# A recurrent layer whose heads run as two chains of 64x64 products, with the modulation beside them

## The chip, the cores and the metric

The kernel runs on one core of one Trainium2 chip. The metric is the device time of one execution in microseconds (us). A core has TensorE (PE in the profile, its weight loads PEld), VectorE (DVE), ScalarE (ACT), GpSimd (POOL) and SyncE (SP), which here issues the transfers (DMA).

## The reference

`reference(...)` runs two blocks one behind the other on 256 tokens of width 1024, in fp32. The first has four layers, each a mixer followed by a gated projection of a side input `p[i]` and a layer norm; the mixers are a short convolution, a state-space layer (S5), the recurrent layer (RWKV-7) and a convolution again. The recurrent layer, with 16 heads of 64, is the one that changes:

```
def _rwkv_step(state, inp):
    r_t, w_t, k_t, v_t, kk_t, a_t = inp
    sa = jnp.einsum("bhvk,bhk->bhv", state, -kk_t)
    state = (state * w_t[:, :, None, :] + sa[..., None] * (kk_t * a_t)[:, :, None, :]
             + v_t[..., None] * k_t[:, :, None, :])
    out = jnp.einsum("bhvk,bhk->bhv", state, r_t)
    return state, out
```

Before it come the projections r, k, v and the low-rank paths for decay and `a`; behind it a norm per head, a bonus term, a gate `silu(z)` and the output product.

The second block has two layers over two streams, the tokens (the first block's output) and a context of 256 rows, which has a feed-forward network (FFN), mixers with attention, and an FFN again. Shifts, scales and gates of both streams come from the **modulation**:

```
        mod_x = jnp.split(jax.nn.silu(c) @ ada_w[l] + ada_b[l], N_MOD, axis=-1)
        mod_c = jnp.split(jax.nn.silu(c_ctx)[None, :] @ ada_w[l] + ada_b[l], N_MOD, axis=-1)
```

## The kernel before, in words

Activations lie transposed in SBUF, 128 channels on the partitions and 256 tokens along the row, in eight such pieces. A linear layer takes its weights in tiles of 128x1024 fp32, 512 KB each, in `get` (L600): SyncE fetches the tile, ScalarE rounds it (`whi`, L601) and VectorE takes the rest (`wlo`, L602); TensorE then runs three products for each 128x128 block, hi by hi, hi by lo, lo by hi, 24 matmuls of 256 columns for a tile. All TensorE products go through `matmul` (L433) or `transpose` (L437), all operations of VectorE and ScalarE but the splits through one helper (L403).

The order on every engine is fixed when the program is written out. Each stream is a Python generator that asks for a weight tile or says how long it would wait; `weave` holds two of them, X (the first block, then the tokens) and C (the context), keeps a model of the engines' times, and lets the stream go on whose operands the model has ready. So C's matmuls fill X's waits. `par` does the same among generators inside a stream. Beside the streams runs `side`, work that is due by the clock of the model, the modulation `ada` above all: for each of 168 tiles of the modulation's weights one transfer of 512 KB (L1376) and one multiplication with a sum along the row for each stream that wants it (L1379, output `junk`, 288 sums). Its core and the condition under which `weave` steps it:

```
while self.side is not None and not self.hold and self.next <= self.now() and (self.V.t < self.now() + SLACK or self.next < self.now() - LATE):
```

`hold` is raised in `square` at the last chunk of a stream's FFN and in the first block's norm, and lowered again in the norm that follows; while it stands, no modulation is issued. `drain` empties the side work on the spot.

The recurrent layer (`rwkv`) works on pairs of heads, two heads on 128 partitions, eight pairs, each in four chunks of 64 tokens. `heads(f)` is the generator for pair f; three run at once, each with its own buffers and its own PSUM tag (`ca`, `cb`, `mm`). For a pair, in order:

- the rates, keys and queries, scaled by the running decay, on VectorE and ScalarE; the r and key rows of each head go into `arz`, zeroed beforehand, so that the other head's 64 rows are zero and products can use all 128 rows (two column halves of PSUM for the two heads);
- the strict lower triangle `lt`, and an inverse `xi` built by doubling in six levels: `lt` by `xi`, copied to `t1` (ScalarE), the transposed inverse `xt` by `t1`, written into `xi` under a mask (VectorE), then `xi` transposed anew by a product with the identity and copied (ScalarE);
- for each of four chunks in sequence: q, xi q, the state, the output, each a product and a copy;
- the norm per head (two sums across partitions as 128x256 products) and the output.

Before the first pair `rwkv` drains the side work; behind the last it drains again and starts the rest of the modulation with a new `ada`.

Of the kernel before, what the change touches and what calls it, by code (L numbers as in the profile page):

```python
# [9 lines left out]
F32 = mybir.dt.float32  # L10
# [3 lines left out]
AF = mybir.ActivationFunctionType  # L14
# [72 lines left out]
def constants():  # L87
# [13 lines left out]
    strict, incl = (s_ < t_) * 1.0, (s_ <= t_) * 1.0  # L101
    c.add("p1mask", np.block([[strict, incl], [strict, incl]]))
    two = lambda m: np.kron(np.eye(2), m)
    c.add("ltmask", two(strict.T))
    c.add("eye", np.tile(np.eye(64), (2, 1)))
    for lv in range(6):
        b = 1 << lv
        m = (s_ // (2 * b) == t_ // (2 * b)) & (s_ // b % 2 == 0) & (t_ // b % 2 == 1)
        c.add(f"lv{lv}", np.tile(m * 1.0, (2, 1)))
    c.add("lvT0", two(((s_ == t_ + 1) & (s_ % 2 == 1)) * 1.0))  # L110
# [329 lines left out]
class Net:  # L440
# [624 lines left out]
    def rwkv(self, X):  # L1065
# [84 lines left out]
        self.drain()  # L1150
        for q in range(3):
            a = self.slot(2 * q, [2048], f"rw_a{q}") if q < 2 else self.big("rw_a2")[:, :2048]
            b = self.slot((1, 3, 10)[q], [2048], f"rw_b{q}")
            s_ = dict(arz=a[:, :1024], bk=a[:, 1024:1792], rate=a[:, 1792:2048], tag=("ca", "cb", "mm")[q])
            s_.update({n: b[:, 512 * i:512 * i + 512] for i, n in enumerate(("lt", "xi", "xt", "t1"))})
            G.memset(s_["arz"], 0.0)
            sets.append(s_)
        free = list(range(3))
# [3 lines left out]
        spare = lambda f: (sets[f % 3]["xi"][:, S:], sets[f % 3]["rate"])  # L1162
# [13 lines left out]
        rates(range(3))  # L1176

        def heads(f):

# [5 lines left out]
            (lw, cw), (ei, _), (kk, sq), (rn, ew) = (two(d[n]) for n in ("lt", "xi", "xt", "t1"))  # L1185
            kv, bt, bv = sq, rn, r[:, f]

# [16 lines left out]

            arz = d["arz"].rearrange("p (c a e t) -> p c a e t", c=4, a=2, e=2)
# [4 lines left out]
            if f % 3 == 2:  # L1210
                rates(range(f + 1, min(f + 4, NCH)))
            V.scalar_tensor_tensor(out=bk[:, :, 0], in0=ch(bt), scalar=0.5, in1=ch(ei), op0=MUL, op1=MUL)
            A.activation(out=bk[:, :, 2], in_=bk[:, :, 0], func=AF.Copy)
            V.tensor_tensor(out=bk[:, :, 1], in0=ch(kv), in1=ch(ei), op=MUL)
            wl = self.few.tile([128, 4], F32, name="wl", bufs=2)
            V.tensor_copy(out=wl, in_=ch(ew)[:, :, 63])
            for e in range(2):
                h = hd[e]
                V.scalar_tensor_tensor(out=arz[h, :, 0, e], in0=ch(kk)[h], scalar=-1.0, in1=ch(lw)[h], op0=MUL, op1=MUL)
                V.tensor_tensor(out=arz[h, :, 1, e], in0=ch(r[:, f])[h], in1=ch(ew)[h], op=MUL)  # L1220
# [3 lines left out]
            for c in range(4):  # L1224
                for e in range(2):
                    T.matmul(vt[hd[e], c * 64:c * 64 + 64], lhsT=svc(c)[:, hv[e]], rhs=self.c("ident")[:, hd[e]], start=True, stop=True)
# [4 lines left out]

            ab2 = lambda t: t.rearrange("p a s -> p (a s)")
            bks = lambda e, c: ab2(bk[:, c, 1 - e:3 - e])
            c4 = lambda t: t.rearrange("p (c t) -> p c t", c=4)
            cm_ = lambda n, k=128: self.c(n, k).unsqueeze(1).to_broadcast([128, 4, k])
            p1 = [c4(d["lt"]), c4(d["t1"])]

            lt, xt, xi, t1 = c4(d["lt"]), c4(d["xt"]), c4(d["xi"][:, :S]), c4(d["t1"][:, :S])
            e4 = lambda t: t.rearrange("p c (e s) -> p c e s", e=2)

            def both(out, f, g):

                for c in range(4):
                    for e in range(2):
                        T.matmul(out[hd[e], c * 64:c * 64 + 64], lhsT=f(c, e), rhs=g(c, e), start=True, stop=True)

            ps = pst()
            pp, pl = two(ps)
            both(pp, lambda c, e: arz[:, c, 0, e], lambda c, e: bk[:, c, 0])
            both(pl, lambda c, e: bk[:, c, 0], lambda c, e: arz[:, c, 0, e])  # L1250
            twice = c4(pp).unsqueeze(2).to_broadcast([128, 4, 2, 64])
            V.tensor_tensor(out=e4(lt), in0=twice, in1=e4(cm_("ltmask")), op=MUL)
            A.activation(out=xi, in_=cm_("eye", 64), func=AF.Copy)
            V.copy_predicated(out=xi, mask=cm_("lv0", 64).bitcast(I32), data=c4(pl))
            A.activation(out=xt, in_=cm_("ident"), func=AF.Copy)
            V.copy_predicated(out=e4(xt), mask=e4(cm_("lvT0")).bitcast(I32), data=twice)
            yield 2.0

            for lv in range(1, 6):
# [3 lines left out]
                yield 0.7  # L1263
                ps = pst()
                both(ps, lambda c, e: xt[:, c, hd[e]], lambda c, e: t1[:, c])
                V.copy_predicated(out=xi, mask=cm_(f"lv{lv}", 64).bitcast(I32), data=c4(ps[:, :S]))
                if lv == 5:
                    break
                yield 0.8
                ps = pst()  # L1270
                for c in range(4):
                    for e in range(2):
# [4 lines left out]
            for e in range(2):  # L1277
                ps = pst()
                for c in range(4):
                    T.matmul(ps[:, c * 128:c * 128 + 128], lhsT=bks(e, c), rhs=arz[:, c, :, e], start=True, stop=True)  # L1280
                V.tensor_tensor(out=p1[e], in0=c4(ps), in1=cm_("p1mask"), op=MUL)

            bkt = d["xt"].rearrange("p (c e t) -> p c e t", c=4, e=2)
            for e in range(2):
                ps = pst()
                for c in range(4):
                    T.transpose(ps[:, c * 64:c * 64 + 64], bks(e, c)[hd[e]], self.c("ident")[hd[e], hd[e]])
                A.activation(out=bkt[:, :, e], in_=c4(ps[:, :S]), func=AF.Copy)
            yield 0.5

            o = d["bk"][:, :S]
            ba, states = d["bk"][:, 256:320], [d["bk"][:, 320 + 64 * i:384 + 64 * i] for i in range(2)]
            state = None
# [679 lines left out]
```

## Time and profile before

| | |
|---|---|
| Median of 3 runs | 2889.77 us (2887.61 to 2893.28) |
| Profiled execution, its own time | 2890.76 us |
| Its span in the trace | 2889.0 us |
| TensorE busy | 2749.4 us, 95% |
| VectorE busy | 2134.0 us, 74% |
| ScalarE busy | 1606.4 us, 56% |
| HBM over the span | 161 GB/s |

The span is the trace's own length, and the execution's time is 1.76 us more. A matmul's end is modelled, so that neighbours overlap; what matters is when the next one starts. A row of the timeline is: start, duration, engine, line, operation, output and inputs with the tile, the count of merged instructions, and in brackets how long the engine had been idle and who ended that. `64*128` before a shape is the rows by columns of the array that a product takes.

### The profile page before, as it was taken

Reading aid. Unit: us, or ns where it says so; the run is one execution under the profiler, and the core shown is the slowest. Engines: PE = TensorE matmul, PEld = TensorE weight load, DVE = VectorE, ACT = ScalarE, POOL = GpSimd, SP = SyncE. Lnnn points to the kernel's source line nnn. Section 1 sums busy time; section 2 is a strip of 40 time slices with the busy share of each in tenths; the row PEclk is TensorE's granted clock in tenths of the full one; section 3 lists DMA queues with packets and bytes.
Section 4 is the critical chain, followed back from the end, with each engine's and each line's share of the span. In section 5 each row is a group of like instructions: output and inputs, shape, how many; then the busy total and the mean of one; then the engine's idle time right before and its main releaser. Section 6 shows DMA issues by size and latency. Waiting matters only on the chain.

```text
span 2889.0 us, 58552 instructions
## 1 busy us (share of the span) xinstructions
PE 2749.4 (95%) x23798; PEld 2604.6 (90%) x23798; DVE 2134.0 (74%) x3953; ACT 1606.4 (56%) x2976; POOL 14.8 (1%) x41
## 2 busy tenths in 40 slices
PE   8978799899999998999999999999999999999999
PEld 8967799778998998998999978999999999996999
DVE  8877777666688788899789887777855556676655
ACT  5455555766555465877666766445422234466443
POOL 0000000000000000000000000000000000000000
PEclk9989799999999999999999999999999999999999
DMA  7743355201586665666576644666543433222554
GB/s 270 238 165 110 108 167 175 82 17 40 163 269 226 220 197 167 209 215 203 182 226 195 199 130 155 203 225 194 180 142 125 139 117 103 89 82 65 161 182 139
DMA packets 132751, 467.53 MB, mean 162 GB/s; under 512 B 14720, under 2 KB 19072, under 8 KB 131840
## 3 DMA queue, kind: packets, MB, share of 16 engines
q1 hardware_dynamic: 132480, 463.78, 50.0%
q8 instruction: 187, 3.06, 0.4%
q14 instruction: 84, 0.69, 0.1%
HBM read 462.67 MB, written 1.05 MB: 161 GB/s over the span
## 4 chain that ended last, share of the span: by engine, by line
PE 72%; DVE 12%; DMA 7%; ACT 6%; issue 3%; SPq 0%; ACTq 0%; DVEq 0%
PE ps_mm L433 62%; PE ps_ca L433 5%; DMA w<-in_ada_dram 5%; DVE wlo L602 3%; PE ps_cb L433 2%; DVE junk L1379 2%; PE ps_st L433 2%; DVE ssm_m L403 2%; ACT whi L601 2%; DVE tc L403 1%; PE ps_cb L437 1%; ACT rw_b L403 1%; ACT L403 1%; ACT tc L403 1%; DMA w<-in_ab_in_dram 1%
## 5 line engine op out<-in xcount | busy, mean ns | idle before, releaser
L601 ACT ACTIVATE whi<-w 128x1024 fp32r<-128x1024 f32 (+1 forms) x687 | 715.9, 1043 | 740.2 <-PE ps_mm L433 488.1
L602 DVE TENSOR_TENSOR wlo<-w,whi 128x1024 fp32r<-128x1024 f32 (+1 forms) x687 | 825.6, 1203 | 239.2 <-ACT whi L601 236.8
L433 PE MATMUL ps_mm<-h_hi,whi 128*128 128x256 f32 x3024 | 873.1, 290 | 17.1 <-ACT h_hi L403 12.4
L433 PE MATMUL ps_mm<-h_hi,wlo 128*128 128x256 f32 x3024 | 859.5, 285 | 9.5 <-DVE wlo L602 9.5
L433 PE MATMUL ps_mm<-h_lo,whi 128*128 128x256 f32 x3024 | 856.5, 284 | 0.6 <-DVE h_lo L403 0.5
L433 PEld LDWEIGHTS ps_mm<-h_hi,whi 128*128 128x128 f32 x3024 | 573.6, 190 | 25.8 <-ACT h_hi L403 15.1
L433 PEld LDWEIGHTS ps_mm<-h_hi,wlo 128*128 128x128 f32 x3024 | 573.3, 190 | 12.2 <-DVE wlo L602 11.5
L433 PEld LDWEIGHTS ps_mm<-h_lo,whi 128*128 128x128 f32 x3024 | 577.5, 191 | 5.2 <-DVE h_lo L403 1.9
L1379 DVE SCALAR_TENSOR_TENSOR junk<-w,cond 128x1024 bf16<-128x1024 f32 x288 | 351.7, 1221 | 145.0 <-DMA w<-in_ada_dram 144.1
L433 PE MATMUL ps_mm<-d_hi,whi 128*128 128x256 f32 x1232 | 355.7, 289 | 4.1 <-DVE ctx L403 3.0
L433 PE MATMUL ps_mm<-d_hi,wlo 128*128 128x256 f32 x1232 | 350.4, 285 | 1.5 <-DVE wlo L602 1.5
L433 PE MATMUL ps_mm<-d_lo,whi 128*128 128x256 f32 x1232 | 349.2, 283 | 0.4 <-DVE d_lo L403 0.4
L433 PEld LDWEIGHTS ps_mm<-d_hi,whi 128*128 128x128 f32 x1232 | 232.3, 189 | 8.7 <-issue 5.7
L433 PEld LDWEIGHTS ps_mm<-d_lo,whi 128*128 128x128 f32 x1232 | 234.0, 190 | 3.4 <-issue 1.2
L433 PEld LDWEIGHTS ps_mm<-d_hi,wlo 128*128 128x128 f32 x1232 | 232.1, 189 | 2.8 <-DVE wlo L602 2.0
L403 DVE TENSOR_TENSOR td<-td,ps_mm 128x256 f32<-128x256 f32 x154 | 64.4, 418 | 70.0 <-PE ps_mm L433 68.9
L403 ACT ACTIVATE d_hi<-td 128x256 fp32r<-128x256 f32 x154 | 63.0, 409 | 89.5 <-DVE td L403 88.7
L403 ACT ACT_TABLE_LOAD x78 | 100.1, 1283 | 2.1 <-PEq L1964 0.7
L433 PE MATMUL ps_mm<-x_hi,whi 128*128 128x256 f32 x256 | 73.5, 287 | 12.0 <-ACT whi L601 12.0
L403 ACT ACTIVATE tc<-tc 128x256 f32<-128x256 f32 x182 | 75.1, 413 | 5.6 <-DVE tc L403 2.6
L433 PE MATMUL ps_mm<-xs_hi,whi 128*128 128x256 f32 x256 | 73.4, 288 | 4.8 <-ACT xs_hi L403 4.4
L403 ACT ACTIVATE td<-ps_mm 128x256 f32<-128x256 f32 x154 | 57.4, 374 | 32.9 <-PE ps_mm L433 32.3
(467 smaller groups left out, 5270.5 us busy)
## 6 DMA issues: line engine op xcount, KB each, us to landing
w<-in_ffn_in_dram SPq DMA_DIRECT2D x268, 512.0 KB, 4.2
w<-in_ada_dram SPq DMA_DIRECT2D x168, 512.0 KB, 4.3
w<-in_ffn_out_dram SPq DMA_DIRECT2D x96, 512.0 KB, 4.1
w<-in_conv_in_dram SPq DMA_DIRECT2D x64, 512.0 KB, 4.7
w<-in_ffn_out_dram SPq DMA_DIRECT2D x48, 384.0 KB, 3.1
w<-in_ab_in_dram SPq DMA_DIRECT2D x34, 512.0 KB, 4.4
w<-in_ple_gate_dram SPq DMA_DIRECT2D x32, 512.0 KB, 4.5
w<-in_conv_out_dram SPq DMA_DIRECT2D x16, 512.0 KB, 5.2
```

Source lines behind the costliest of these rows:

```text
L403: return f(**kw)
L433: self.t.matmul(out, lhsT=lhsT, rhs=rhs, start=start, stop=stop)
L437: self.t.transpose(out, in_, ident)
L601: nc.scalar.activation(out=hi[:, :n], in_=w[:, :n], func=AF.Copy)
L602: nc.vector.tensor_tensor(out=lo[:, :n], in0=w[:, :n], in1=hi[:, :n].bitcast(F32), op=ALU.subtract)
L1379: nc.vector.scalar_tensor_tensor(out=self.junk, in0=w, scalar=1.0, in1=cb[:, s], op0=ALU.mult, op1=ALU.mult, accum_out=m[:, t, s:s + 1])
```

## The change

- There are two sets of buffers and two heads' pairs at a time instead of three. `arz` with its zeros becomes `ar`, and every product of a pair takes a 64x64 quadrant (or 64x128) of the array, the head's own rows.
- The inverse is kept with its transpose: `x` is updated at each level by a second set of products, under masks `lvT0` to `lvT4`, and no product with the identity stands between levels.
- The four chunks' sequence is cut into steps that do all chunks at once (U, the two products with the inverse `zy` and `py`, the states' parts, the outputs); two short steps for the states alone are in sequence.
- `ada` takes its tiles one by one from a shared list, `todo`; the drain ahead of the heads is gone, so that it goes on beside them, and behind the heads a second `ada` takes up the same list. The list has the parts of before in the same order with the same gaps.

```
         sets = []
-        self.drain()
-        for q in range(3):
-            a = self.slot(2 * q, [2048], f"rw_a{q}") if q < 2 else self.big("rw_a2")[:, :2048]
...
-            G.memset(s_["arz"], 0.0)
-            sets.append(s_)
-        free = list(range(3))
+        for q in range(2):
+            a, b = (self.slot(2 * q + i, [2048], f"rw_{'ab'[i]}{q}") for i in range(2))
...
+        free = list(range(2))
...
             for lv in range(1, 6):
-                ps = pst()
-                both(ps, lambda c, e: lt[:, c, hd[e]], lambda c, e: xi[:, c])
-                A.activation(out=t1, in_=c4(ps[:, :S]), func=AF.Copy)
+                ps = [pst(), pst()]
+                for j, p, e in four:
+                    mm(ps[e][hd[p], j * 64:j * 64 + 64], lt[hd[e], 2 * j + p], xi[hd[e], 2 * j + p])
+                A.activation(out=t1[:, 0], in_=ju(ps[0]), func=AF.Copy)
+                V.tensor_copy(out=t1[:, 1], in_=ju(ps[1]))
                 yield 0.7
-                ps = pst()
-                both(ps, lambda c, e: xt[:, c, hd[e]], lambda c, e: t1[:, c])
-                V.copy_predicated(out=xi, mask=cm_(f"lv{lv}", 64).bitcast(I32), data=c4(ps[:, :S]))
-                if lv == 5:
-                    break
-                yield 0.8
-                ps = pst()
-                for c in range(4):
-                    for e in range(2):
-                        T.matmul(ps[hd[e], c * 64:c * 64 + 64], lhsT=xi[:, c], rhs=self.c("ident")[:, hd[e]], start=True, stop=True)
-                for e in range(2):
-                    A.activation(out=xt[hd[e], :, hd[e]], in_=c4(ps[:, :S])[hd[e]], func=AF.Copy)
-                yield 0.9
+                ps = [pst(), pst()]
+                for j, p, e in four:
+                    mm(ps[p][hd[e], j * 64:j * 64 + 64], x[hd[p], e, j], t1[hd[p], e, j])
+                if lv < 5:
+                    for j, p, e in four:
+                        at = 128 + 128 * e + 64 * j
+                        mm(ps[p][hd[p], at:at + 64], t1[hd[p], e, j], x[hd[p], e, j])
+                for p in range(2):
+                    V.copy_predicated(out=xi[:, p::2], mask=imask(f"lv{lv}", 2), data=ju(ps[p]))
+                if lv < 5:
+                    for p in range(2):
+                        V.copy_predicated(out=ch(B[1])[hd[p]], mask=imask(f"lvT{lv}")[hd[p]], data=ch(ps[p][:, 128:384])[hd[p]])
+                yield 0.8
...
-            for c in range(4):
-                v = svc(c)
...
+            zy, py = pst(), pst()
+            for c in range(4):
+                for e in range(2):
+                    mm(zy[op[e], c * 128:c * 128 + 128], xi[hd[e], c], ua[hd[e], c])
...
+            for c in range(1, 3):
                 ps = pst()
...
-        yield from self.par((heads(f) for f in range(NCH)), 3)
+        yield from self.par((heads(f) for f in range(NCH)), 2)
         self.fine = False
-        self.drain()
-        self.side, self.next = self.ada(self.slot(13, [2 * D], "cond1"), [(0, i, (0,), GAPS[1] / 2) for i in range(PARTS)] + [(0, i, (0, 1), GAPS[1]) for i in range(PARTS, 9)] + [(1, i, (0, 1), GAPS[2 + (i > 2)]) for i in range(9)]), self.now()
+        self.side, self.next = self.ada(self.slot(13, [2 * D], "cond1"), self.todo), self.now()
...
-    def ada(self, cond, parts):
+    def ada(self, cond, todo):
...
-        for l, i, streams, gap in parts:
+        while todo:
+            l, i, t, streams, gap = todo.pop(0)
             m = self.mod[:, l, i * NCH:(i + 1) * NCH]
-            for t in range(NCH):
-                w = self.ws.tile([128, D], F32, name="w")
-                nc.sync.dma_start(out=w, in_=self.ap[f"ada{l}"][i * NCH + t])
+            w = self.ws.tile([128, D], F32, name="w")
+            nc.sync.dma_start(out=w, in_=self.ap[f"ada{l}"][i * NCH + t])
```

How the order moves is seen at two places. The first is TensorE inside the inverse (`rw_b` holds a pair's `xi`, `lt`, `xt`, `t1`; `ps_ca`, `ps_cb` and `ps_mm` are the chains' PSUM tiles, `cs_base` holds the identity). Before, with three chains:

```order
L433 MATMUL ps_mm<-rw_b_5708 64x64 x2
L433 MATMUL ps_ca<-cs_base,rw_b_5702 64x64 x8
L433 MATMUL ps_cb<-cs_base,rw_b_5705 64x64 x8
L433 MATMUL ps_ca<-rw_b_5702 64x64 x8
L433 MATMUL ps_cb<-rw_b_5705 64x64 x8
```

After, with two, in the second half of the heads:

```order
L434 MATMUL ps_ca<-rw_b_5826 64x64 x15
L434 MATMUL ps_cb<-rw_b_5828 64x64 x9
L434 MATMUL ps_ca<-rw_b_5826 64x64 x8
L434 MATMUL ps_cb<-rw_b_5828 64x64 x15
L434 MATMUL ps_ca<-rw_b_5826 64x64 x16
```

A level's three groups of eight products (the one with `cs_base` and two of `rw_b` alone) have become eight and sixteen, the group with `cs_base` is gone, and there is no third chain; no linear product stands between them. The second place is SyncE's queue of transfers from the end of the heads on. Before, the loads of the z projection alternate with the modulation's (`in_ada`), and tiles of the context's FFN (`in_ffn`) stand among them:

```order
L1370 DMA cond_8953<-in_cond_dram 128x2048
L600 DMA w<-in_ffn_in_dram 128x1024 x3
L1376 DMA w<-in_ada_dram 128x1024 x3
L600 DMA w<-in_rwkv_z_dram 128x1024 x2
L1376 DMA w<-in_ada_dram 128x1024
```

After:

```order
L601 DMA w<-in_ffn_out_dram 128x768 x2
L511 DMA second<-in_const_second_dram 128x2304
L601 DMA w<-in_rwkv_z_dram 128x1024 x8
L1409 DMA cond_10637<-in_cond_dram 128x2048
L601 DMA w<-in_rwkv_out_dram 128x1024 x8
L601 DMA w<-in_ple_proj_dram 128x1024 x2
L601 DMA w<-in_ple_gate_dram 128x1024 x8
L601 DMA w<-in_conv_in_dram 128x1024 x32
L601 DMA w<-in_conv_out_dram 128x1024 x6
```

The context's FFN has its last tile ahead of z (`in_ffn_out ... 128x768`), and X's loads follow each other with no tile of the modulation or of the context between them, up to the end of the fourth layer. Over all, the heads stage (from the first product of the heads to the z projection) holds 3047 rows of products in place of 2007; 1224 linear products of the context's FFN in place of 408; 23 tiles of the modulation in place of two; and 262 changes of the array's tile shape in place of 228. From z to the tokens 808 linear products of the context's FFN have gone. Modulation tiles issued by the time r is projected are 43 in place of 24, by the first head 54 in place of 24, at z 77 in place of 27, at the first token projection 78 in place of 65. COPY_PREDICATED rises from 84 to 196 in all.

## Rows read from the trace of the kernel before

**Rows 1.** The page: span, and busy time of each engine

```profile
span 2889.0 us, 58552 instructions
PE 2749.4 (95%) x23798; PEld 2604.6 (90%) x23798; DVE 2134.0 (74%) x3953; ACT 1606.4 (56%) x2976; POOL 14.8 (1%) x41
```

**Rows 2.** Stretches: length, busy us of each engine, PEclk (granted clock), DMA share, GB/s

```profile
450.60:529.20 78.60, 77.36 (x648) 76.12 (x646) 55.53 (x92) 53.84 (x111) 2.06 (x2) 1.00 0.58 180
529.20:772.10 242.90, 226.07 (x3526) 191.46 (x3522) 153.03 (x369) 153.96 (x419) 0.00 (x0) 0.98 0.17 52
772.10:1115.20 343.10, 327.93 (x2658) 323.53 (x2656) 284.77 (x491) 194.94 (x323) 1.45 (x6) 0.99 0.67 220
1115.20:1300.00 184.80, 175.97 (x1330) 169.41 (x1330) 164.50 (x307) 135.09 (x247) 0.00 (x0) 0.97 0.64 206
174.30:193.30 19.00, 4.99 (x12) 2.65 (x10) 12.74 (x33) 13.14 (x31) 0.00 (x0) 0.63 0.35 121
863.50:884.70 21.20, 14.69 (x109) 13.46 (x108) 19.41 (x42) 13.16 (x26) 0.00 (x0) 0.94 0.66 217
```

**Rows 3.** The chain in order of time: start, us, what; one long piece

```profile
1809.03 200.32 PE ps_mm L433 x1648
```

**Rows 4.** TensorE's timeline in the heads: one level of the inverse

```profile
564.32 0.69 PE L433 MATMUL ps_ca<-rw_b 128*64 128x64 f32 x16 [0.70 <-ACT rw_b L403]
564.83 0.64 PE L433 MATMUL ps_cb<-rw_b 128*64 128x64 f32 x16
565.30 0.29 PE L433 MATMUL ps_mm<-rw_b 128*64 128x64 f32 x4
565.55 0.69 PE L433 MATMUL ps_ca<-cs_base,rw_b 128*64 128x64 f32 x16
...
568.40 0.69 PE L433 MATMUL ps_ca<-rw_b 128*64 128x64 f32 x16 [0.76 <-ACT rw_b L403]
```

**Rows 5.** TensorE's timeline in the state-space layer: products of 32 rows

```profile
200.29 0.27 PE L433 MATMUL ps_ca<-ta,bT 32*128 32x128 f32 x1
200.31 0.27 PE L433 MATMUL ps_cb<-ta,bT 32*128 32x128 f32 x1
200.40 0.27 PE L433 MATMUL ps_ca<-ta,bT 32*128 32x128 f32 x1
```

**Rows 6.** TensorE's timeline in the heads: products of a 64x64 quadrant

```profile
583.78 0.46 PE L437 MATMUL ps_cb<-cs_base,rw_a 64*128 64x64 f32 x4 [0.15 <-ACT rw_b L403]
584.16 0.33 PE L433 MATMUL ps_ca<-rw_a,rw_b 64*64 64x64 f32 x4
584.43 0.34 PE L433 MATMUL ps_cb<-sv,rw_b 128*64 128x64 f32 x4
```

**Rows 7.** Groups of VectorE in the heads: busy, mean ns, idle before and releaser

```profile
L602 DVE TENSOR_TENSOR wlo<-w,whi 128x1024 fp32r<-128x1024 f32 x17 | 20.8, 1224 | 8.8 <-ACT whi L601 8.7
L403 DVE COPY_PREDICATED rw_b<-rwkv_c,ps_ca 128x256 f32<-128x256 int32 x18 | 8.0, 442 | 13.9 <-PE ps_ca L433 13.7
```

**Rows 8.** Stretches, the modulation's sums alone: length, busy us and count on VectorE

```profile
529.00:772.00 243.00, 2.25 (x3) 0.98 0.17 52
772.00:1115.00 343.00, 60.52 (x100) 0.99 0.67 221
```

**Rows 9.** The page: the modulation's sums over the whole span

```profile
L1379 DVE SCALAR_TENSOR_TENSOR junk<-w,cond 128x1024 bf16<-128x1024 f32 x288 | 351.7, 1221 | 145.0 <-DMA w<-in_ada_dram 144.1
```

**Rows 10.** TensorE's timeline in the first layer's norm

```profile
178.34 0.70 PE L433 MATMUL ps_st<-total,cs_base 128*128 128x256 f32 x2 [3.90 <-DVE total L403]
179.13 1.22 PE L433 MATMUL ps_st<-r,cs_base 128*128 128x256 f32 x2
186.96 2.93 PE L433 MATMUL ps_st<-sq,cs_base 128*128 128x256 f32 x6 [6.61 <-DVE sq L403]
193.33 4.88 PE L433 MATMUL ps_mm<-x,w 128*128 128x256 f32 x15 [3.44 <-ACT x L403]
```

**Rows 11.** TensorE's timeline where the first convolution's output product begins

```profile
119.58 0.38 PE L433 MATMUL ps_mm<-g_hi,whi 128*128 128x256 f32 x1 [2.16 <-ACT g_hi L403]
```

More of the change, by code (lines that the diff above doesn't have):

```diff
@@ L1184, in heads @@
             hv = [slice(f * 128 + 64 * e, f * 128 + 64 * e + 64) for e in range(2)]
-            (lw, cw), (ei, _), (kk, sq), (rn, ew) = (two(d[n]) for n in ("lt", "xi", "xt", "t1"))
+            B = d["b"]
+            lw, cw, ei, kk, sq, rn, ew = (B[i] for i in (0, 1, 2, 4, 5, 6, 7))
             kv, bt, bv = sq, rn, r[:, f]
+            mm = lambda out, lhsT, rhs, start=True, stop=True: T.matmul(out, lhsT=lhsT, rhs=rhs, start=start, stop=stop, share=4)
             tw, th = spare(f)
@@ L1277, in heads @@
[L1277 to L1293, printed above, removed]
-            for c in range(4):
-                v = svc(c)
+            lt, xi = ch(B[0]), ch(B[2])
+            ej = lambda t: t.rearrange("p (e j t) -> p e j t", e=2, j=2)
+            x, t1 = ej(B[1]), ej(B[4])
+            four = [(j, p, e) for j in range(2) for p in range(2) for e in range(2)]
+            mask = lambda n, k=4: self.c(n, 64).unsqueeze(1).to_broadcast([128, k, 64])
@@ L1296, in heads @@
+            for c in range(1, 3):
                 ps = pst()
                 for e in range(2):
-                    q = ps[hd[e], 0:64]
-                    T.matmul(q, lhsT=p1[e][:, c, 0:64], rhs=v[:, hv[e]], start=True, stop=state is None)
-                    if state is not None:
-                        T.matmul(q, lhsT=arz[:, c, 0, e], rhs=state, start=False, stop=True)
-                A.activation(out=ba, in_=ps[:, 0:64], func=AF.Copy)
+                    mm(ps[hd[e], :64], mt[hd[e], c], states[c - 1][hd[e]])
+                V.scalar_tensor_tensor(out=states[c], in0=ps[:, :64], scalar=wl[:, c:c + 1], in1=states[c], op0=MUL, op1=ADD)
@@ L1303, in heads @@
                 yield 0.6
-                ps = pst()
+            ps = pst()
+            for c in range(1, 4):
                 for e in range(2):
-                    T.matmul(ps[op[e], 0:64], lhsT=xi[hd[e], c], rhs=ba[hd[e]], start=True, stop=True)
+                    mm(ps[op[e], c * 64:c * 64 + 64], yt[hd[e], c], states[c - 1][hd[e]])
+            pc = ch(ps[:, :S])
+            for i in range(2):
                 for e in range(2):
-                    A.activation(out=v[op[e], hv[e]], in_=ps[op[e], 0:64], func=AF.Copy)
@@ L1320, in heads @@
-                ps = pst()
-                for e in range(2):
-                    q = ps[hd[e], 0:64]
-                    T.matmul(q, lhsT=v[:, hv[e]], rhs=p1[e][:, c, 64:128], start=True, stop=state is None)
-                    if state is not None:
-                        T.matmul(q, lhsT=state, rhs=arz[:, c, 1, e], start=False, stop=True)
-                A.activation(out=o[:, c * 64:c * 64 + 64], in_=ps[:, 0:64], func=AF.Copy)
-                state = new
-                yield 0.6
-            sq, rn = two(d["lt"])
+                    t = sv[i][op[e], 1 - i:, hv[e]]
@@ L1923, in load_context @@
             yield 1.0
-        n.side = itertools.chain(n.ssm_prep(), load_context(), n.ada(c, [(0, i, (1,), GAPS[0] / 2) for i in range(PARTS)]))
+        one, both = (0,), (0, 1)
+        ninths = [(0, i, (1,), GAPS[0] / 2) for i in range(PARTS)] + [(0, i, one, GAPS[1] / 2) for i in range(PARTS)] + [(0, i, both, GAPS[1]) for i in range(PARTS, 9)] + [(1, i, both, GAPS[2 + (i > 2)]) for i in range(9)]
+        n.todo = [(l, i, t, streams, gap) for l, i, streams, gap in ninths for t in range(NCH)]
+        n.side = itertools.chain(n.ssm_prep(), load_context(), n.ada(c, n.todo))
         n.weave([X], lambda: n.parts[0][1] > 1 and n.stage != "")
```

167 lines of the change are left out of this document (110 added, 57 removed).

## The prediction

> **What bounds the kernel now.** I read the page's totals first [rows 1]: TensorE is busy 2749.4 of 2889.0 us, so 140 us at most are open to any change that leaves TensorE's work alone. This change leaves nearly all of it alone, so the question is where TensorE waits, before and after. Next, the busy time by stretches [rows 2], cut where a first matmul of a stage starts: 450.6 the layer's projections, 529.2 the heads, 772.1 the z projection, 1115.2 the first token matmul. The reader is to see that the heads stretch has the lowest TensorE share (226.07 of 242.90) with VectorE busy only 153.03, and that the stretch behind it is dense (327.93 of 343.10). "Busy" hides slow stretches, so I count by start spacing instead: the chain has 1648 linear matmuls back to back in 200.32 us, 0.1216 us each [rows 3]; single weight tiles of 24 go at 0.1195 to 0.1216. I use 0.1195, or 2.87 us for a tile.
>
> In the heads stretch the order of the program has 408 context-FFN matmuls, 49 us. The head products are read in the timeline [rows 4]: 16 records (8 fp32 products, two passes each) start 0.46 to 0.52 us after the 16 before, 0.0585 us a product, since the two column halves run together. Going from whole rows to another tile shape costs about 0.12 us more than that (four records take 0.25 us from 565.30 to 565.55); I estimate 0.115. The order has 228 such switches, 26 us. The dense head work comes to 133 us by the same prices, so 242.9 = 49 + 133 + 26 + 35 of loss. The loss is seen in the inverse: a level repeats every 4.08 us (564.32, then 568.40), each wait of 0.70 to 0.76 us ended by ScalarE's copy of a PSUM result; three such round trips make a level, about 1.36 us each.
>
> **Products in quadrants.** Two bounds per 64x64 product. Below: four lanes on different rows and columns start 10 ns apart and the next four 0.11 us later [rows 5], which gives 0.029 us a product. Above: no gain on column pairs, 0.0585 us. The before kernel has one kind of quadrant pair [rows 6]: four records at 584.16 from two quadrants, the next start 0.27 us later, switch included, so two run together. I take 0.029 for the 960 products that the change writes four quadrants in turn (the inverse) and 0.0585 for the other 624, which alternate two; with transposes and the 47 fp32 head sums, unchanged, that is 129 us, against 133. Switches rise to 262, 30 us. So TensorE saves nothing on balance: 159 against 159 us. All products at 0.0585 would add 28 us, all at 0.029 would take 18 off.
>
> **The levels.** A level loses one of three round trips (the transpose), but gains three predicated copies (two of the level, two of the kept transpose, for one). One 128x256 copy took 442 ns [rows 7]. From 4.08 us: 2/3 of it is 2.7, and half of the three extra copies is hidden by the other chain, so about 3.2 us for a level with both chains. The four chunks' q, xi, state, out sequence becomes some nine batched steps of 1.4 to 2 us. A round of two heads alone I put at 52 us (47 to 59) against 40 us of TensorE work.
>
> **The filler moves.** This is the part the diff does not show. The order puts 1224 context-FFN matmuls (146 us) into the heads, up from 408, all in the first two of four rounds; the last two rounds hold head products alone. First two rounds: TensorE 146 + 80 = 226, about 240 with waits. Last two: 2 x 52 = 105. Heads after: **345 us**. Before, with the same 816 matmuls more at 0.1195, it is 242.9 + 97.5 = 340.4. The heads alone: **+4.5** (from -19 with both halves nearly dense, to +40).
>
> **Beside the heads** come 23 modulation tiles, 46 sums of 1.22 us, where three sums ran before [rows 8, 9]. VectorE's work there, back to back, comes to about 285 us of 345: 149 for the heads' own operations, 63 for some 55 weight splits at 1.14 (the 1224 ns of [rows 7] less overlap), 53 for sums, 21 for the FFN. It fits, so I cost it at nothing; its cover is the 60 us that are left.
>
> **Ahead of the heads** 17 sums more enter a stretch where VectorE had 55.53 of 78.60 us busy [rows 2]: 19 us into 23, a nearly full engine. With a burst of five tiles after the state-space layer: **+3**.
>
> **Behind the heads.** 808 FFN matmuls and 50 tiles' sums (x100 [rows 8]) leave the 343.1 us stretch. The flag that stops the side work at the end of the context FFN now stands through the whole stretch, so neither filler nor modulation runs there. What did the filler cover? A norm: without cover it takes 19.0 us of which TensorE waits 14 in three pieces (3.90, 6.61, 3.44 [rows 10]), at a granted clock of 0.63 [rows 2], between its two levels; the covered one takes 21.2 us with 96 FFN matmuls (11.5 us) inside, so 9.7 net. Two norms lose 9.4 each, 19; a stage's start, whose first matmul waits 2.16 us for its operand where nothing covers it [rows 11], about 2.3 three times, 7. So **+25** on a stretch whose loss was 343.1 - 2632 x 0.1195 - 7.7 = 21. Ends: +10 if loads that now run far ahead make up for it, +35 if the slow clock lasts into the matmuls behind.
>
> **Tokens.** Six held-back modulation tiles go at once in front of the first token projections: **+2**. Behind that some 13 tiles fewer are left for a stretch where VectorE is busy 164.50 of 184.80 us [rows 2]; the gaps set their pace, so I give **-3**.
>
> Sum: 3 + 4.5 + 25 + 2 - 3 = +31.5 on the profiled 2890.8 us, and the median of the runs is 1 us below that: **2921 us**.
>
> A rule against this change: the Trainium skill, "TensorEngine Tiling (Array Packing)", section Gotcha 1: PSUM Pressure, says that different row tiles cannot use one PSUM bank at the same time. By it the 448 products that put two row tiles into one bank would go one after the other, about +30 us. The trace's pair at 584.16, two row tiles into one tile of PSUM, started 7 ns apart.
>
> **Rivals.** *A, the heads go dense.* If quadrants cost 0.029 throughout and the two chains cover each other, the heads take 18 us less TensorE work and most of the 35 us of loss: 345 falls to about 305, and the total to about 2880, **faster**. For: pairs of chains overlapped well in rows 4. Against: two chains without filler have 40 us of work against chain steps of 47 or more. It decides where a round without filler falls under 43 us. Chance 0.18. *B, nothing on balance*: heads about 318 and +10 behind them, 2886 to 2896. Chance 0.10. *C, evacuation binds:* a batched step ends in VectorE copies, and a sum of 1.22 us or a split stands in front of each; with some 40 chain steps a round and half a piece before every third, 0.6 x 13 x 4 = 32 us more: 2955. For: VectorE at 285 of 345. Against: ScalarE takes part of the copies. Chance 0.14. The same section's neighbour, PSUM Bottleneck, on the Trainium skill's page "TensorEngine Tiling (Array Packing)", says that tiling speeds TensorE and not the emptying of PSUM; that is C. *D, the bank rule above:* two row tiles into one bank in sequence, priced from rows as 448 products at 0.0585 more, +26: 2947. Chance 0.05, since the pair in rows 6 ran together. *Forecast:* 0.53, its own range 2903 to 2945.
>
> **Numbers.** A measurement of this kernel can tell about 0.2%, 5.8 us. Faster by more: A, 0.18; within: B, 0.10; slower: forecast, C and D, 0.72. The range takes in A's centre and C's: 2868 to 2960.
>
> **What would show it.** Right: the heads stretch at 330 to 360 us, its second half with no linear matmul and TensorE waiting for copies; z to the first token matmul at about 270 us, with two waits of 14 us of norm and a granted clock near 0.63 in them; modulation sums in the heads, none between z and the tokens. Wrong: a round of two heads without filler under 43 us; four quadrants starting together for all products; the norms' waits in the third layer no longer than before; or time saved behind the tokens, where I see only 3 us.

## The result, and the profile after

The changed kernel takes 2938.89 us in the median (2936.07 to 2942.81, 4 runs) against 2890.43 us before: a ratio of 1.0172, 95% interval 1.0160 to 1.0185. It is slower by 1.7%. The forecast was 2921 us, slower by 1.1%.

The page of the changed kernel's profile, span and busy times (the counterpart of [rows 1]), and the modulation's sums over the whole span (of [rows 9]):

```profile
span 2936.3 us, 59597 instructions
PE 2759.0 (94%) x24246; PEld 2603.4 (89%) x24246; DVE 2181.3 (74%) x4161; ACT 1564.6 (53%) x2839; POOL 11.8 (0%) x38
L1418 DVE SCALAR_TENSOR_TENSOR junk<-w,cond 128x1024 bf16<-128x1024 f32 x288 | 351.4, 1220 | 103.5 <-DMA w<-in_ada_dram 102.8
```

TensorE is busy 9.6 us longer, and waits some 38 us longer. Below, **filler** is the context FFN's matmuls, which stand in the waits of the other stream. The stretches of the changed kernel, columns as in [rows 2]: the projections; the heads with filler (536.8 to the context FFN's last matmul at 778.0); the heads without; from the heads to the first token product; the tail of that, the fourth layer's norm:

```profile
458.30:536.80 78.50, 75.14 (x627) 74.72 (x626) 71.70 (x123) 52.44 (x109) 0.00 (x0) 1.00 0.74 246
536.80:778.00 241.20, 232.68 (x2978) 212.83 (x2976) 217.27 (x482) 118.67 (x226) 0.00 (x0) 0.98 0.53 174
778.00:906.80 128.80, 104.00 (x1834) 81.76 (x1833) 89.89 (x275) 48.03 (x129) 0.00 (x0) 0.86 0.05 19
906.80:1180.30 273.50, 237.91 (x1854) 230.60 (x1853) 192.91 (x329) 144.90 (x252) 1.47 (x6) 0.91 0.49 159
1152.50:1180.30 27.80, 8.55 (x20) 4.98 (x20) 27.65 (x63) 16.63 (x38) 0.00 (x0) 0.58 0.44 137
```

For every run below the same two stretches are compared, the heads (first to last product of the heads) and what is behind them (to the first token product), and for each the **net** time: the stretch less its context-FFN matmuls at 0.1195 us. Before, the heads take 245.8 us from 526.3 with 408 such matmuls, net 197.0, and the stretch behind 343.1 with 808, net 246.5. Changed: 370.0 with 1224, net 223.7, and 273.5 with none. By step, against before: ahead of the heads +10.5 us, of which 2.9 are 24 context matmuls that come earlier, so +7.6; heads net +26.7; behind net +27.0; from the tokens on 1750.0 against 1768.3 less 3.8 for 32 matmuls, -14.5. The moved matmuls cancel; the four make 46.8 of the 47.3 us between the spans, and the rest lies behind the last product.

The modulation's sums alone in the changed kernel, columns as in [rows 8]; a sum shows as two instructions here, so x92 are 46 sums (and the x100 of [rows 8] are 50 sums, not 50 tiles' as the prediction wrote, its x3 two sums and not three):

```profile
458.00:537.00 79.00, 20.68 (x34) 1.00 0.74 246
537.00:778.00 241.00, 56.42 (x92) 0.98 0.53 174
778.00:907.00 129.00, 0.00 (x0) 0.86 0.05 19
907.00:1180.00 273.00, 15.26 (x25) 0.91 0.49 160
1180.00:2936.00 1756.00, 208.28 (x340) 1.00 0.48 155
1152.50:1180.30 27.80, 10.65 (x17) 0.58 0.44 137
```

The last row is the tail ahead of the tokens: nine of the 13 sums behind the heads stand in it.

The second half of the heads has neither filler nor sums. Its slices, columns as in [rows 2]:

```profile
778.00:800.00 22.00, 18.95 (x205) 13.61 (x203) 16.82 (x47) 10.22 (x24) 0.00 (x0) 0.69 0.14 50
800.00:840.00 40.00, 33.83 (x724) 27.52 (x724) 28.66 (x92) 14.11 (x42) 0.00 (x0) 1.00 0.01 3
840.00:870.00 30.00, 20.65 (x332) 16.10 (x334) 22.10 (x70) 10.79 (x33) 0.00 (x0) 0.72 0.01 1
870.00:890.00 20.00, 17.66 (x410) 14.78 (x404) 14.66 (x45) 4.12 (x15) 0.00 (x0) 1.00 0.01 3
890.00:906.80 16.80, 12.92 (x176) 9.76 (x175) 7.65 (x25) 8.78 (x18) 0.00 (x0) 0.82 0.18 64
```

The granted clock is full in the inverses (800 to 840, 870 to 890), 0.69 and 0.72 where two pairs begin together, and 0.82 at the end. These are means over the two levels of 1.2 and 2.4 GHz; the first slice, cut where the level changes:

```profile
778.00:784.80 6.80, 4.38 (x53) 2.76 (x51) 6.64 (x22) 3.79 (x9) 0.00 (x0) 1.00 0.01 5
784.80:798.50 13.70, 13.37 (x136) 10.19 (x136) 8.72 (x23) 4.95 (x13) 0.00 (x0) 0.50 0.17 62
```

What happens where two pairs begin is read from the chain in time (start, us, what) of the changed kernel from 854 us on: one VectorE operation after the other, the first ten of a row of 17 (to 860.2 us), with hardly anything for TensorE to do.

```profile
854.18 1.20 DVE rw_b L404 x3
855.38 0.33 DVE tc L404
855.71 0.33 DVE rw_b L404
856.04 0.34 DVE tc L404
856.37 0.33 DVE rw_b L404
856.71 0.40 DVE rw_a L404
857.10 0.35 DVE tc L404
857.46 0.40 DVE r L404
```

TensorE's timeline of the changed kernel: a level of the inverse at full clock (806.82, and the next at 809.95), the first product group of a pair, and the waits of the fourth layer's norm into the tokens (the counterparts of [rows 4], [rows 6] and [rows 10]):

```profile
785.13 1.97 PE L434 MATMUL ps_ca<-rw_a 64*64 64x64 f32 x32 [0.80 <-DVE rw_a L404]
...
806.82 0.92 PE L434 MATMUL ps_ca<-rw_b 64*64 64x64 f32 x16 [0.26 <-DVE rw_b L404]
...
808.12 0.75 PE L434 MATMUL ps_ca<-rw_b 64*64 64x64 f32 x26
808.67 0.27 PE L434 MATMUL ps_cb<-rw_b 64*64 64x64 f32 x2
808.71 0.28 PE L434 MATMUL ps_ca<-rw_b 64*64 64x64 f32 x3
...
809.95 0.27 PE L434 MATMUL ps_ca<-rw_b 64*64 64x64 f32 x2 [0.20 <-DVE rw_b L404]
...
1154.93 0.70 PE L434 MATMUL ps_st<-total,cs_base 128*128 128x256 f32 x2 [2.19 <-DVE total L404]
1156.75 1.13 PE L434 MATMUL ps_st<-r,cs_base 128*128 128x256 f32 x2 [1.12 <-DVE r L404]
1162.38 2.92 PE L434 MATMUL ps_st<-sq,cs_base 128*128 128x256 f32 x6 [4.51 <-DVE sq L404]
1167.41 2.08 PE L434 MATMUL ps_st<-squares,cs_base 128*128 128x256 f32 x4 [2.10 <-DVE tc L404]
1178.81 2.08 PE L434 MATMUL ps_mm<-squares,cs_base 128*128 128x256 f32 x4 [9.32 <-DVE squares L404]
```

A level takes 3.13 us in place of 4.08. In the norm no filler covers TensorE's waits, every one of them ended by VectorE, which is busy 27.65 of the 27.80 us there, 10.65 of them with sums.

### The profile page after: what moved, and what is told of

It reads as the page before. It is cut to its first block, busy times and chain, and to the rows that moved or that the text cites. A ratio compares the mean times of both kernels' runs of the same rounds, so it can differ in the third digit from the quotient of the medians.

```text
span 2936.3 us, 59597 instructions
## 1 busy us (share of the span) xinstructions
PE 2759.0 (94%) x24246; PEld 2603.4 (89%) x24246; DVE 2181.3 (74%) x4161; ACT 1564.6 (53%) x2839; POOL 11.8 (0%) x38
## 4 chain that ended last, share of the span: by engine, by line
PE 60%; DVE 9%; ACT 5%; DMA 3%; issue 2%; DVEq 0%; ACTq 0%; SPq 0%
PE ps_mm L434 52%; PE ps_ca L434 4%; PE ps_cb L434 2%; DVE wlo L603 2%; DMA w<-in_ada_dram 2%; DVE junk L1418 2%; ACT whi L602 1%; PE ps_st L434 1%; DVE rw_b L404 1%; DVE tc L404 1%; PE ps_cb L438 1%; ACT tc L404 1%; ACT L404 1%; ACT L395 1%; DVE rw_a L404 0%
## 5 line engine op out<-in xcount | busy, mean ns | idle before, releaser
L434 PE MATMUL ps_mm<-h_hi,whi 128*128 128x256 f32 x3024 | 871.6, 290 | 13.7 <-ACT h_hi L404 8.2
```

Of the source, the lines that this page charges most:

```text
L434: self.t.matmul(out, lhsT=lhsT, rhs=rhs, start=start, stop=stop)
```

## The experiments

Each run's times are against the kernel before on the same chip.

**1. The filler spread over all pairs.** A floor between two of the context's weight tiles while the heads run:

```
+    def due(self):
+        return max(self.ready, self.net.pace) if self.cache is not None and self.net.gap and isinstance(self.req, tuple) else self.ready
...
+                self.net.pace = self.net.now() + self.net.gap
...
-            s = next((s for s in live if s.ready <= self.now()), None)
+            s = next((s for s in live if s.due() <= self.now()), None)
...
         self.fine = FINE & 2
+        self.gap = 8.0
```

> The changed kernel with one thing else: a floor of 8 us (model time) between two weight tiles of the context's FFN while the heads run, so that its products are spread over all eight pairs of heads (about 100 to 120 in each eighth instead of 300 in the first four and none in the last four), and 450 instead of 96 context products are left for the stretch between the heads and the tokens. Theory 1 (the loss is where the filler lies: the last four pairs run alone and the norms are bare): heads from 370 us to about 290, the stretch behind from 273 to about 300, median about 2890 (2875 to 2905). Theory 2 (the new products and copies themselves cost more than the old ones): the filler only changes place, 2925 to 2940. Theory 3 (the modulation beside the heads holds VectorE, and with it every chain step): the same VectorE work, 2920 to 2940.

Measured: 2933.93 us, 1.0162 (1.0141 to 1.0183). Theory 1 fell in this form. Behind the heads the filler worked: 354 matmuls (42.3 us) cost 22.6 us there (296.1 against 273.5), net 253.8. But the heads, with 870 matmuls, took 342.1 us, net 238.1, worse than with the filler in one half. With the filler spread, 70 sums stood in the heads, and not 46.

**2. The new heads with the modulation as before.**

```
+        self.drain()
         for q in range(2):
...
-        n.todo = [(l, i, t, streams, gap) for l, i, streams, gap in ninths for t in range(NCH)]
...
+        todo = [(l, i, t, streams, gap) for l, i, streams, gap in ninths for t in range(NCH)]
+        n.todo, todo = todo[PARTS * NCH:], todo[:PARTS * NCH]
...
```

> One part alone: the new heads with two chains, but the modulation as before (drained ahead of the heads, taken up again behind them). The order then spreads 1190 context products evenly over the heads, with nothing on VectorE beside them. Theory 1: no pair runs alone, heads about 320 us, the stretch behind stays bare of filler but has modulation again; 2895 to 2910. Theory 2: heads stay at 350 or more, 2920 to 2940. Theory 3: heads about 310 to 320 too, 2885 to 2905; it is the run with spread filler and the modulation kept that tells theory 3 from theory 1.

Measured: 2951.22 us, 1.0218 (1.0203 to 1.0233), outside all three. The heads were as theories 1 and 3 had them but for the size, 334.7 us with 1191 matmuls, net 192.4. The time went behind them, 329.7 us with 57. Its timeline around the tokens:

```profile
1139.15 2.08 PE L434 MATMUL ps_mm<-squares,cs_base 128*128 128x256 f32 x4 [15.27 <-DVE squares L404]
1187.67 0.58 PE L434 MATMUL ps_mm<-h_hi,whi 128*128 128x256 f32 x1 [46.45 <-ACT h_hi L404]
```

and the sums alone in the two stretches ahead of that product:

```profile
862.00:1108.00 246.00, 7.38 (x12) 0.97 0.50 173
1108.00:1188.00 80.00, 64.62 (x105) 0.54 0.72 239
```

The context's FFN ended soon behind the heads (57 matmuls were left), so the flag stood from there on; the tokens' own modulation was still to do, and came in one burst of 53 sums, with TensorE waiting 46.45 us behind it.

**3. The old products, with two chains and the modulation beside them.** The kernel before, with `range(3)` of the sets and the width of `par` made 2, no drains, and the shared list.

> The other part alone: the heads' products of the kernel before (128 rows, a transpose in each level, chunks in sequence), but two chains and the modulation beside them from the shared list. The order has 1100 context products over all pairs and 220 behind. Theory 1: heads about 310 to 330 us, since filler covers the third round trip, stretch behind about 285; 2900 to 2920. Theory 2: the old products are the cheaper ones, 2885 to 2900. Theory 3: VectorE has the same modulation and fewer copies, 2920 to 2940.

Measured: 2954.99 us, 1.0227 (1.0208 to 1.0245), slower than any theory had it. Heads 354.3 us with 1101 matmuls, net 222.7, behind net 272.9. These two nets are close to those of the changed kernel (223.7 and 273.5), but not under the same conditions: here the filler lies over all pairs and 78 sums stand in the heads. Nearer to it in both is run 1, which has the new products, 70 sums and a net of 238.1, 15 us more. No run sets old and new products against each other in one order.

**4. The flag lowered while the context waits for the tokens.**

```
+            n.hold -= 1
             yield from n.wait("tokens")
+            n.hold += 1
```

> The changed kernel with one thing else: the flag that stops the modulation is lowered while the context waits for the tokens, so that modulation tiles run in the third and fourth layer again. Theory 1: they are no cover for TensorE, whose waits in the norms are ended by VectorE; no gain, 2930 to 2945. Rival (the six tiles in one burst ahead of the tokens and the dense modulation behind them are what costs): 2915 to 2928.

Measured: 2974.21 us, 1.0299 (1.0283 to 1.0314), worse than either. 27 sums now came into the second half of the heads, where nothing but the chains ran:

```profile
778.00:925.00 147.00, 113.67 (x1798) 88.54 (x1796) 118.65 (x325) 49.92 (x128) 0.00 (x0) 0.76 0.22 78
925.00:1207.90 282.90, 240.89 (x1855) 232.49 (x1853) 227.11 (x400) 145.05 (x250) 1.46 (x6) 0.89 0.55 187
```

147.0 us in place of 128.8, at a granted clock of 0.76, and 282.9 behind in place of 273.5. A sum beside a bare chain costs some 0.7 us (18.2 over 27), if all of that is put down to it: the planner books these sums too, and the order of the chains' steps changes with them.

**5. The new products alone**, three chains and the modulation as before:

```
-        for q in range(2):
-            a, b = (self.slot(2 * q + i, [2048], f"rw_{'ab'[i]}{q}") for i in range(2))
...
+        self.drain()
+        for q in range(3):
+            a = self.slot(2 * q, [2048], f"rw_a{q}") if q < 2 else self.big("rw_a2")[:, :2048]
+            b = self.slot((1, 3, 10)[q], [2048], f"rw_b{q}")
...
-        yield from self.par((heads(f) for f in range(NCH)), 2)
+        yield from self.par((heads(f) for f in range(NCH)), 3)
...
```

> The new products alone: three chains of heads as in the kernel before (the third set of buffers and the third PSUM tag again) and the modulation as before, drained ahead of the heads; so only the quadrants, the kept transpose and the batched chunks differ from before. Theory A (the loss comes from two chains that start in step, with VectorE alone at work in their beginnings, and from the filler's place): three chains shift against each other, heads net of the context's products from 193 us to about 175 to 185; median 2870 to 2885. Theory B (the new heads need as much TensorE time as the old ones, and switches of tile shape eat what quadrants give): 2885 to 2900. Theory C (the added predicated copies and copies on VectorE bind): over 2900.

Measured: 2887.95 us, 0.9993 (0.9982 to 1.0004): no difference from before. Heads 279.1 us with 768 matmuls, net 187.3, some 10 less than before and a little short of theory A's 175 to 185; behind, 480 matmuls and net 264.2, 18 more; the total is theory B's. What the products save in the heads goes back in the stretch behind, from which the heads took filler. Part of that is again a burst ahead of the tokens, whose first product waits 13.2 us (TensorE's waits behind the heads, and the sums from 1090 us on):

```profile
PE ps_mm L434 <- ACT h_hi L404: 13.2, 1, 13.2
1090.00:1124.00 34.00, 22.20 (x37) 0.65 0.51 170
```

**6. Spread filler in whole weight tiles, no modulation beside the heads.** Run 1 with `self.fine = False` and the flag raised over the heads.

> The changed kernel with the filler spread as in the first run (8 us between weight tiles), but the context's matmuls put in whole weight tiles of 24 instead of pieces of 12 in the heads, and no modulation during the heads. Theory A: heads about 280 us with some 740 context products in them (net 190), stretch behind 285, the tokens as in the changed kernel or up to 10 us longer for the 23 tiles that move there: 2865 to 2890. Theory B: fewer switches than the 361 of the first run, net 185 to 200, the same range, upper half. Theory C: VectorE has the same copies, net over 205, above 2895.

Measured: 2897.57 us, 1.0028 (1.0014 to 1.0043). Heads 282.9 us with 741 matmuls, net 194.4: the net of theories A and B, the total of C. The trace shows 358 changes of tile shape there, as many as run 1's 361, so these were not run 1's trouble.

**7. A control: the kernel before with whole weight tiles in the heads.**

```
-        self.fine = FINE & 2
+        self.fine = False
```

> A control: the kernel before, with the context's matmuls in the heads in whole weight tiles instead of pieces of 12. Theory B: some switches of tile shape less, 0 to 8 us faster, 2882 to 2890. Otherwise no difference, 2887 to 2893, or slower by some us since larger pieces stand in front of chain steps.

Measured: 2888.62 us, 0.9998 (0.9987 to 1.0009): no difference, though 253 of the context's matmuls moved into the heads, 220 of them from the stretch behind (net 193.5 and 257.1).

**8. The changed kernel without modulation during the heads** (`self.hold += 1` ahead of `par`, `-= 1` behind it).

> The changed kernel without modulation during the heads (the flag raised while they run); the order then puts the 1224 context products evenly into all eight pairs by itself. Theory A: no pair alone, heads from 370 to about 340, 2905 to 2920. Theory C (VectorE binds): the same or more, as 46 sums of 1.2 us are gone: 2890 to 2915. Theory B: the filler only changes its place among pairs, more switches: 2925 to 2940.

Measured: 2917.16 us, 1.0091 (1.0070 to 1.0111). With the same 1224 matmuls, now even over the pairs, the heads took 332.6 us, net 186.3, 37 less than in the changed kernel, with the clock at full level in both halves:

```profile
538.60:704.00 165.40, 159.69 (x2438) 138.73 (x2436) 128.82 (x331) 95.62 (x195) 0.00 (x0) 1.00 0.25 83
704.00:871.20 167.20, 158.71 (x2375) 138.09 (x2372) 124.70 (x313) 95.73 (x181) 0.00 (x0) 0.99 0.30 99
```

Of these 37 us the whole kernel keeps some 22: the stretch behind takes 280.8 us in place of 273.5, and the tokens' part 6.7 more, with the tiles that moved there. Was it VectorE's load that went, or the filler's place that changed? Run 9 tells.

**9. The order kept, the sums left out.** While the heads run, `ada` books its time with the planner (the model of the engines' times) as it does in the changed kernel, but issues no load and no sum; these modulation values stay zero:

```
...
+            if not self.skip:
+                w = self.ws.tile([128, D], F32, name="w")
+                nc.sync.dma_start(out=w, in_=self.ap[f"ada{l}"][i * NCH + t])
             for s in streams:
                 self.V.any_time(1.13)
+                if not self.skip:
...
```

> The changed kernel with its order kept, but the 23 modulation tiles that stand beside the heads left out (their loads and 46 sums are not issued and those modulation values stay zero; the planner still books their time). So the filler stands as in the changed kernel, all in the first four pairs, and only VectorE's load differs. Theory A (the sums act through the planner: they push the filler into the first half and leave the last four pairs alone): heads 360 to 370 us against 370, last half about 125 to 129 us as before; median 2925 to 2938. Theory C (the sums stand in front of the chain's steps on VectorE): heads about 335, 2895 to 2910.

Measured: 2936.47 us, 1.0167 (1.0146 to 1.0187), as theory A had it. Its two halves of the heads:

```profile
537.50:774.60 237.10, 229.88 (x2978) 210.16 (x2976) 165.69 (x369) 117.61 (x226) 0.00 (x0) 0.98 0.35 118
774.60:902.30 127.70, 102.54 (x1835) 80.12 (x1833) 89.77 (x275) 47.94 (x129) 0.00 (x0) 0.88 0.05 19
```

VectorE is busy 165.69 us in the first half in place of 217.27, and the heads take 364.8 us in place of 370.0. So the sums themselves, with their loads, cost some 5 us in this order (one trace each; the ratios of the whole kernels, 1.0167 and 1.0172, do not tell the two apart). Runs 8 and 9 have the same products, the same 1224 matmuls and no sums in the heads, and differ in the order alone: 332.6 against 364.8, **32 us**. The filler's place is what differs most in that order (600 and 624 matmuls in the halves of run 8, 1224 and none in run 9). The chains' steps are interleaved otherwise too, and no run moves the filler with their order kept.

**10. Run 6 with the modulation beside the heads again.**

> The run with the filler spread in whole weight tiles, with the modulation beside the heads again. Theory A: with the filler even, the sums cost little: heads net of the context's products 195 to 210 us, median 2900 to 2912. Theory C: net 225 to 240 as in the first run, 2920 to 2940. The first run's net of 238 then comes from the sums and not from the 361 switches of tile shape.

Measured: 2925.16 us, 1.0133 (1.0110 to 1.0155), theory C's numbers: heads 344.0 us with 931 matmuls, net 232.7. VectorE in the heads of this run, by groups:

```profile
L1426 DVE SCALAR_TENSOR_TENSOR junk<-w,cond 128x1024 bf16<-128x1024 f32 x72 | 87.5, 1216 | 0.3
L609 DVE TENSOR_TENSOR wlo<-w,whi 128x1024 fp32r<-128x1024 f32 x41 | 49.6, 1214 | 0.6 <-ACT whi L608 0.4
```

72 sums, where the changed kernel has 46, and VectorE busy 307.59 of 344.0 us. Net 38 us more than run 6: TensorE waits 31.7 us in place of 11.0, and the mean granted clock is 0.95 in place of 1.00. That is 0.5 us a sum, but not the sums' own cost alone: by their bookings the order changes as well (931 context matmuls in place of 741), and no run here leaves the sums out of this order.

**11 and 12. Three chains with a floor**, run 5 with the floor of run 1 at 8 and at 6 us.

> Three chains of the new heads, the modulation drained ahead of them as before, and the floor of 8 us between weight tiles in the heads, so that some 720 context products are left for the stretch behind, nearly as many as before (808). Theory A: heads net 185 to 195 us as with three chains before, the stretch behind net about 247 as before, no wait for a burst of modulation ahead of the tokens (20 us in the run with three chains): 2865 to 2880, the fastest. Theory B (the new heads need as much time as the old): 2882 to 2892.

Measured: 2901.92 us, 1.0051 (1.0035 to 1.0066), slower than either theory. Behind the heads net 246.1, as before; but the heads net 202.2 with 499 matmuls, and the tokens' part 21 us longer than in run 5 (1776.9 against 1755.9), 3.8 of them for 32 context matmuls still to do when the tokens begin.

> Between the two runs with three chains: a floor of 6 us between weight tiles in the heads instead of none or 8, so that about 600 context products are left for the stretch behind (480 and 717 in those two). Theory A (there is a best place for the filler, and three chains with it beat both kernels): heads net about 192 us, stretch behind net about 253, the tokens as in the run without a floor; 2872 to 2884. Theory B (what the filler gives at one place it takes at another, and the new heads themselves give nothing): 2885 to 2900.

Measured: 2889.89 us, 1.0012 (1.0003 to 1.0022): heads net 193.5 with 647, behind net 258.6 with 601, theory B's total. No place for the filler was found that beats the kernel before.

## Why the prediction was right, and where it was not

The forecast case came true: slower, and by the mechanism that carried it, the place of the filler. Of the 47 us the heads' net has 27, which three nets put together: 186.3 with the filler even and no sums (run 8), 218.5 with the changed kernel's order and no sums (run 9), 223.7 with the sums, against 197.0 before. The stretch behind has another 27. That the total came within 18 us of the forecast is in part luck: the heads cost 22 us more than forecast, and the tokens' part 13.5 less. Step by step:

- **Products in quadrants: nothing on balance.** True of the whole kernel (run 5 is 0.9993 of before), not of the heads: there run 5's net is 10 us less, and TensorE, less the context matmuls, is busy some 166 us in place of 180 (257.9 with 768 of them against 228.3 with 408, over the two heads stretches), where the forecast had 159 twice. One price was wrong the other way: of the 960 products taken at 0.029 us, the 256 that update the kept transpose alternate two quadrants only. In the trace the level's first 16 records from 808.12 on start four at a time (within 0.02 us, the later fours 0.058 us apart), those from 808.42 on in pairs 0.058 us apart. At the forecast's own 0.0585 these 256 cost 7.5 us more over the heads (an estimate). At a level the forecast of 3.2 us stands against 3.13; its own terms add up to 3.4, and the new copies, half as wide, take 0.357 us (mean of 42 in the second half) and not 0.442.
- **Heads, first two rounds: 240 us.** 241.2 measured. **Last two: 105 us** was the step that failed: 128.8. TensorE waits 24.8 us in it (128.80 less 104.00), just the 25 that the forecast had. What was mis-sized is the 80 us of products: TensorE is busy 104.0. The sum took every product at full clock, while two pairs that begin in step leave TensorE idle behind VectorE's chain, and the granted clock of the half is 0.86. In the stretches at 1.2 GHz, 36.8 us in all, TensorE is busy 32.2 us. A pair of 128x256 records takes 1.02 us there (789.49 to 790.51) and 0.54 at 2.4 GHz (835.01 to 835.55), so up to 16 of the 24 us are the clock's, and 4 the kept transpose's (estimates); the rest stays open. No run separates these, and a version that only shifts the two chains against each other was not tried.
- **Beside the heads: nothing.** Right for VectorE's load (5 us by run 9; it is busy 307 of 370 us, where the forecast had 285 of 345), wrong as a whole: the planner books the sums, by these bookings the order puts the filler into the first half, and that order costs 32 us (runs 8 and 9). These 32 us lie inside the heads' time, where the forecast had the filler's place already; it did not see the modulation as its cause. Rival C, sums in front of the chains' steps, is not shown by itself: runs 4 and 10 lose 0.5 to 0.7 us a sum, the changed order included.
- **Behind the heads: +25.** +27.0 measured, with the norm's waits bare and the granted clock at 0.58 in the last 27.8 us. That filler there pays is shown by run 1 (42.3 us of it for 22.6) and run 11 (net 246.1 with 717). But the size is not the bare norms' alone: nine sums stand in the last norm, part of the burst that the forecast had booked with the tokens (+2), and the third layer's norm without any (990.5 to 1006.2) has 11.1 us of waits and not 14.
- **Ahead: +3, tokens: +2 and -3.** +7.6 and -14.5. Of the 7.6, 4.9 lie ahead of the projections, where 20 more sums stand, and 2.7 in them. The tokens' part has 43 sums fewer (x340 against x426) and no context FFN left; its order changes too, and run 11 shows that this part moves by 17 us with the order, beside its 32 matmuls, so the 14 are not settled. Time saved behind the tokens was one of the prediction's own signs of being wrong, and it came. Of its signs of being right, the second half without a linear matmul and the norms' bare waits came; the heads at 330 to 360 us and no sums between z and the tokens did not (370, and 13 sums).
- **Rival A** (heads dense) asked for a half without filler under 43 us a round; it took 64. **Rival B**'s own terms (heads 318, +10 behind) add up to some 2879 and not to 2886 to 2896; the heads, at 370, rule it out. **Rival D**, the bank rule: the 32 records at 785.13 belong to products of two row tiles in one PSUM tile; the trace has them start in pairs 7 ns apart, 16 pairs in the 1.9 us to the next group (at 1.2 GHz), 0.12 us a pair. Each lane's next record starts 0.107 us later, so one at a time they would take about twice that (an estimate). The rule of the Trainium skill, "TensorEngine Tiling (Array Packing)", Gotcha 1: PSUM Pressure, that different row tiles cannot use one PSUM bank at the same time, is not borne out as a cost for these products.

## What to carry to other kernels

Filler is worth what it covers, not where it fits: 42 us of matmuls cost 23 beside bare norms (run 1), and 30 us of them cost 27 in the heads of the kernel before, where TensorE is busy 228 of 246 us already (run 7), so count what a change takes from the stretch behind. In a statically planned kernel, side work acts twice, by its own time and by the time the planner books for it; leaving it out while the order is kept separates the two. Two chains that begin in step stand on the same engine at once. Here that showed in the half without filler: with filler under all pairs two chains took net 186.3 us (run 8), three 187.3 (run 5). Work that is held back by a flag comes as a burst: in run 2 TensorE waited 46 us behind one.

## What was not expected of the hardware

The granted clock fell within the heads' second half: after 6.8 us at 2.4 GHz in which TensorE was busy 4.38 us (778.0 to 784.8), it stood at 1.2 GHz for 13.7 us in which TensorE was busy 13.37, and was back at 2.4 GHz in the inverses (1.00 from 800 to 840). A busy share read over the whole slice, 18.95 of 22.00 us, hides this: the half-speed products fill the time. The inverse's small products start at the spacing of both of the prediction's bounds, by how many quadrants they take in turn: from 808.12 to 808.71, 28 records (14 products) start in 0.59 us, 0.042 us a product on the mean, some 0.029 with four quadrants and 0.058 with two.
